# Block transposes and a way over DRAM in place of 32 TensorE transposes, in a hybrid decoder layer

## The chip, the cores and the metric

The kernel runs on one core of one Trainium2 chip. The metric is the device time of one execution in microseconds (us), here the median of three runs. A core has TensorE (PE; its weight loads are listed as PEld), VectorE (DVE), ScalarE (ACT), GpSimd (POOL) and SyncE (SP), and 16 DMA engines that they share. TensorE writes only to PSUM, which has eight banks here, two for each of the tags acc, s, pt and o.

## The reference

One decoder layer over 1040 tokens (16 learned meta tokens ahead of 1024 tokens) of width 1024:

```python
h = concat([meta, x])                               # (1040, 1024)
u = rmsnorm(h, g_pre_mix)
q, k, v, xr, yr = split(u @ w_in)                   # widths 512, 128, 128, 512, 512
attn = sliding_window_attention_with_sinks(q, k, v) # window 128, 8 heads, 2 kv heads
hr = rg_lru(causal_depthwise_conv(xr))              # gated linear recurrence over time
rec = gelu(yr) * hr
h = h + rmsnorm(concat([attn, rec]) @ w_out, g_post_mix)
f = square(relu(rmsnorm(h, g_pre_ffn) @ w_ff1)) @ w_ff2
out = (h + rmsnorm(f, g_post_ffn))[16:]
```

All inputs and outputs are float32.

## The kernel before

Every float32 operand of a matrix product is split into a high part (rounded to float32r, ScalarE) and a low part (the remainder, VectorE). A product is three matmuls, high by high, high by low and low by high (`mm3`, lines 125, 130 and 131), added up in one PSUM bank.

The change lies in the first stage, the input projection. Its right-hand operand is `u`, kept transposed: eight pairs of tiles (one for each 128 columns of the width, index `kc`), 1040 tokens wide. It is made in four pieces of tokens, `ALL = [(0, 272), (272, 256), (528, 256), (784, 256)]`. Piece 0 holds the meta tokens and x tiles 0 and 1 (128 tokens each); piece `b` holds x tiles `2b` and `2b + 1`. The x tiles are loaded early by SyncE into eight buffers of tag c (`load_x`, line 147), which later hold other things.

To make a piece, `norm_rows` (line 254 the square with its sum on ScalarE, lines 170 and 176 the power on POOL, line 260 the scaling on VectorE) writes a normalised tile into one of four buffers of tag d. `transposed` (line 357) then has TensorE transpose each 128x128 block of it against an identity matrix into a PSUM bank, the tags pt, o and s in turn, and `split_scaled` (lines 117 and 118) evicts the bank with the gain `g_pre_mix` as the scale: ScalarE writes the high part of `u`, VectorE the low part.

The loop over `b` at line 498 then runs four projections on each piece: k, v, the first pair of q heads and the first quarter of x_rec, each 24 matmuls of 256 columns into an acc bank (`project`, `part`), with an eviction (`sink_k` line 433 and 437, `sink_v` 464, `sink_q` 476 and 479, `sink_x` 490). `done[b]` keeps the transposes of piece `b` behind the projections of piece `b - 2`, in order alone.

The order of instructions on each engine is not written by hand. A planner simulates the program and picks, for each engine, the ready instruction with the highest priority (program order, with a few exceptions); it also adds every semaphore. Buffers of one tag are handed out as they come free. On the chip each engine then runs its list in order, and SyncE's DMAs are issued in the order of its list. After the first stage SyncE loads the weights of later projections (line 208) and the gate weights (line 794).

Of the kernel before, what the change touches and what calls it, by code (L numbers as in the profile page):

```python
# [9 lines left out]
F32 = mybir.dt.float32  # L10
F32R = mybir.dt.float32r
AF = mybir.ActivationFunctionType
ALU = mybir.AluOpType
# [3 lines left out]
P = 128  # L17
D = 1024
KC = D // P
# [18 lines left out]
def hybrid_layer(  # L38
# [6 lines left out]
    nc = tc.nc  # L45
# [4 lines left out]
    small = ctx.enter_context(tc.tile_pool(name="small", bufs=4))  # L50
    slab = ctx.enter_context(tc.tile_pool(name="slab", bufs=1))
    ps = ctx.enter_context(tc.tile_pool(name="ps", bufs=2, space=PSUM))
    dpool = ctx.enter_context(tc.tile_pool(name="dpool", bufs=1, space=DRAM))
# [4 lines left out]
    def slot(tag, shape, dt=F32):  # L58
        uid[0] += 1
        return slab.tile(shape, dt, tag=tag, name=f"{tag}{uid[0]}", bufs=bufs[tag])  # L60

    def pair(tag, shape):
        return slot(tag, shape, F32R), slot(tag, shape, F32R)

    def bank(tag, shape=(P, 512)):
        uid[0] += 1
        return ps.tile(list(shape), F32, tag=tag, name=f"ps_{tag}{uid[0]}")

    def f32(ap):
        return ap.bitcast(F32)  # L70
# [35 lines left out]
    def behind(name, *inss):  # L106
        for ins in inss:
            tc.add_manual_dep(
                ins, name,
                mybir.DependencyInfo(  # L110
                    mybir.DependencyClass.NoSync, mybir.DependencyReason.DATA
                ),
                reason="order",
            )

    def split_scaled(hi, lo, src, scale):
        high = nc.scalar.activation(hi, src, AF.Copy, scale=scale).ins
        low = nc.vector.scalar_tensor_tensor(
            lo, src, scale, f32(hi), op0=ALU.mult, op1=ALU.subtract
        ).ins  # L120
        return high, low
# [21 lines left out]
    xt = []  # L143
# [18 lines left out]
    g_mix_col, g_ffn_col = gcol[:, 0:8], gcol[:, 8:16]  # L162
# [4 lines left out]
    def rstd_of(ssq_parts, n=P):  # L167
        ms = small.tile([P, 1], F32, name="ms", tag="ms")
        if len(ssq_parts) == 1:
            nc.gpsimd.tensor_scalar(ms[:n], ssq_parts[0], EPS, None, op0=ALU.add)  # L170
        else:
            nc.vector.scalar_tensor_tensor(
                ms[:n], ssq_parts[0], EPS, ssq_parts[1], op0=ALU.add, op1=ALU.add
            )
        rs = small.tile([P, 1], F32, name="rs", tag="rs")
        last_pow[0] = nc.gpsimd.tensor_tensor(
            rs[:n], ms[:n], half_pow[:n], op=ALU.pow
        ).ins.name
        return rs[:n]
# [49 lines left out]
    u = [pair("a", [P, TT]) for _ in range(KC)]  # L229
    RMS_SC = 1.0 / math.sqrt(D)  # L230

    def norm_first(src, halves):

        xn = slot("d", [P, D])
        ss = [small.tile([P, 1], F32, name=f"hq{i}", tag=f"hq{i}") for i in range(2)]
        c = slice(0, 512 if halves else D)
        nc.scalar.activation(
            xn[:, c], src[:, c], AF.Square, scale=RMS_SC, accum_out=ss[0]
        )
        if halves:  # L240
            c = slice(512, D)
            nc.vector.tensor_tensor_reduce(
                out=xn[:, c], in0=src[:, c], in1=src[:, c], scale=RMS_SC * RMS_SC,
                scalar=EPS, op0=ALU.mult, op1=ALU.add, accum_out=ss[1],
            )
        rs = root_rstd(ss[0], ss[1] if halves else eps_col)
        for c in (slice(0, 512), slice(512, D)):
            nc.vector.tensor_scalar(xn[:, c], src[:, c], rs, None, op0=ALU.mult)
        return xn

    def norm_rows(src, n, link=False):
        xn = slot("d", [P, D])
        ssq = small.tile([P, 1], F32, name="ssq", tag="ssq")
        ins = nc.scalar.activation(
            xn[:n], src, AF.Square, scale=RMS_SC, accum_out=ssq[:n]
        ).ins
        if link:
            chained(0, ins)
        rs = rstd_of([ssq[:n]], n)
        ins = nc.vector.tensor_scalar(xn[:n], src, rs, None, op0=ALU.mult).ins  # L260
        if link:
            chained(1, ins)
        return xn
# [24 lines left out]
    ALL = [(0, 272), (272, 256), (528, 256), (784, 256)]  # L288
# [17 lines left out]
    def load(n, cols, after=None):  # L306
        for _ in range(n):
            ins = nc.tensor.matmul(
                idle[:, :cols], zeros[:, :P], zeros[:, :cols], start=True, stop=True,
                skip_group_check=True,  # L310
            ).ins
            if after:
                behind(after, ins)
        return ins.name
# [4 lines left out]
    def normed(b):  # L319
        if b == 0:  # L320
            return [
                (norm_rows(meta_t[:NMETA], NMETA), NMETA),
                (norm_first(xt[0], True), P), (norm_first(xt[1], False), P),
            ]
        rows = [(xt[2 * b], P), (xt[2 * b + 1], P)]
        return [(norm_rows(s[:m], m), m) for s, m in rows]
# [4 lines left out]
    def chained(e, ins):  # L331
        if last[e] is not None:
            behind(last[e], ins)
        last[e] = ins.name
# [12 lines left out]
    def low_w(w, raw):  # L347
        chained(1, nc.vector.tensor_tensor(w[1], raw, f32(w[0]), op=ALU.subtract).ins)

    def transposed(b, xn, after=None):  # L350
        t0, n = ALL[b]
        for kc in range(KC):
            flip[0] += 1
            pt = bank(("pt", "o", "s")[flip[0] % 3])
            o = 0
            for s, m in xn:
                ins = nc.tensor.transpose(
                    pt[:, o : o + m], s[:m, kc * P : (kc + 1) * P], ident[:m, :m]
                )
                if after:  # L360
                    behind(after, ins.ins)
                o += m
            if b == 0:
                load(1, P, ins.ins.name)
            uh, ul = u[kc]
            if b == 0 and kc in (0, 1):
                key_casts.pop(0)()
            high = split_scaled(
                uh[:, t0 : t0 + n], ul[:, t0 : t0 + n], pt[:, :n],
                g_mix_col[:, kc : kc + 1],  # L370
            )
            if b == 0:
                chained(0, high[0])
                chained(1, high[1])

    def fetch(cols, tag="raw", pieces=1):
        raw = slot(tag, [P, KC, P])
        o = 0
        for lo, n in cols:
            src = w_in[:, lo : lo + n].rearrange("(k p) c -> p k c", p=P)  # L380
            for i in range(pieces):
                ks = slice(KC // pieces * i, KC // pieces * (i + 1))
                nc.sync.dma_start(raw[:, ks, o : o + n], src[:, ks])
            o += n
        return raw
# [6 lines left out]
    xn = normed(0)  # L392
# [70 lines left out]
    def sink_v(acc, t0, n):  # L463
        ins = nc.scalar.copy(vt[:, t0 : t0 + n], acc).ins
        if t0 == 0:
            chained(0, ins)
# [28 lines left out]
    done = [None, None]  # L495
    q0, sink_q0 = new_q()
    xr0, sink_x0 = new_x("c")
    for b in range(4):
        if b:
            transposed(b, xn if b == 1 else normed(b), done[b])  # L500
        piece = ALL[b]
        if b == 0:

            acc = [bank("acc"), bank("acc")]
            for a, w in zip(acc, (wk, wv)):
                part(a, w, piece, 0)
                part(a, w, piece, 1)
            xn = [(norm_rows(xt[2], P, True), P)]
            xn.append((norm_rows(xt[3], P, True), P))
            part(acc[0], wk, piece, 2)  # L510
            sink_k(acc[0][:, : piece[1]], *piece)
            part(acc[1], wv, piece, 2)
            sink_v(acc[1][:, : piece[1]], *piece)
            wx = high_w(rx)
            low_w(wx, rx)
            for w, (t0, n), sink, tag in (
                (wq, (16, 256), sink_q0, "o"), (wx, piece, sink_x0, "acc"),
            ):
                acc = bank(tag)
                for k in range(3):  # L520
                    part(acc, w, (t0, n), k)
                sink(acc[:, :n], t0, n)
            done.append(last_mm[0])
            continue
        project(wk, [piece], sink_k)
        project(wv, [piece], sink_v)
        project(wq, [piece], sink_q0)
        project(wx, [piece], sink_x0)
        done.append(last_mm[0])
    for h in range(2):  # L530
        r, o, m = HALF[h], HALF[1 - h], slice(P - NMETA, 2 * P)
# [62 lines left out]
    for b in range(2):  # L594
        pv = bank("pt", (P, 4, P))
        for i in range(4):
            o = NMETA + (4 * b + i) * P
# [288 lines left out]
    for cs in ((0, 1), (2, 3)):  # L886
# [13 lines left out]
        for c in cs:  # L900
            for half in range(2):
                y = ys[c][:, 512 * half : 512 * half + 512]
# [400 lines left out]
    done = set()  # L1303
# [205 lines left out]
```

## Time and profile before

| what | value |
|---|---|
| device time, median of 3 runs | 956.22 us (954.28 to 958.12) |
| span of the profiled execution | 955.3 us |
| device time of the profiled execution | not given apart from its span |
| bytes from and to HBM | 109.93 MB read, 18.87 MB written |
| DMAs issued by SyncE between 28 and 65 us | none |

The span runs from the first to the last instruction of the profiled execution. Busy time is the time that an engine had an instruction at work; a line number is that of the source line (often of a helper) that issued it. In the timeline each row gives the start, the duration and the operation, and in brackets the idle time ahead of it with what ended it.

### The profile page before, as it was taken

Reading aid. Unit: us, or ns where it says so; the run is one execution under the profiler, and the core shown is the slowest. Engines: PE = TensorE matmul, PEld = TensorE weight load, DVE = VectorE, ACT = ScalarE, POOL = GpSimd, SP = SyncE. Lnnn points to the kernel's source line nnn. Section 1 sums busy time; section 2 is a strip of 40 time slices with the busy share of each in tenths; the row PEclk is TensorE's granted clock in tenths of the full one; section 3 lists DMA queues with packets and bytes.
Section 4 is the critical chain, followed back from the end, with each engine's and each line's share of the span. In section 5 each row is a group of like instructions: output and inputs, shape, how many; then the busy total and the mean of one; then the engine's idle time right before and its main releaser. Section 6 shows DMA issues by size and latency. Waiting matters only on the chain.

```text
span 955.3 us, 12432 instructions
## 1 busy us (share of the span) xinstructions
PE 943.8 (99%) x4728; PEld 789.7 (83%) x4728; DVE 655.7 (69%) x845; ACT 505.9 (53%) x854; POOL 129.1 (14%) x189
## 2 busy tenths in 40 slices
PE   9999999999999999999999999999999999999996
PEld 8999999877888878888888888888887788888885
DVE  6567987788856787665644465476667576779893
ACT  7537766568645554444655575654433343446441
POOL 4102563520021100010000000001121100001201
PEclk9999999999999999999999999999999999999999
DMA  8221010204226368674422364334777765647934
GB/s 271 56 67 23 24 45 24 67 23 131 83 109 185 133 220 264 198 253 144 155 89 88 111 203 127 104 113 114 175 180 186 185 199 177 192 139 196 246 65 89
DMA packets 88199, 130.21 MB, mean 136 GB/s; under 512 B 13702, under 2 KB 52630, under 8 KB 88140
## 3 DMA queue, kind: packets, MB, share of 16 engines
q1 hardware_dynamic: 78972, 104.44, 34.0%
q0 software_dynamic: 8880, 24.19, 12.2%
q8 instruction: 37, 0.61, 0.3%
q10 hardware_dynamic: 288, 0.79, 0.2%
q14 instruction: 22, 0.18, 0.1%
HBM read 109.93 MB, written 18.87 MB: 135 GB/s over the span
## 4 chain that ended last, share of the span: by engine, by line
PE 88%; DVE 5%; ACT 3%; DMA 2%; POOL 1%; issue 1%; SPq 0%; DVEq 0%; ACTq 0%; POOLq 0%
PE ps_acc L130 10%; PE ps_acc L131 10%; PE ps_acc L125 10%; PE ps_s L131 6%; PE ps_s L130 6%; PE ps_s L125 6%; PE ps_pt L130 6%; PE ps_pt L131 6%; PE ps_pt L125 6%; PE ps_o L130 5%; PE ps_o L131 5%; PE ps_o L125 5%; ACT c L82 1%; PE ps_o L691 1%; PE ps_acc L282 1%
## 5 line engine op out<-in xcount | busy, mean ns | idle before, releaser
L99 DVE TENSOR_TENSOR ws<-raw,ws 128x1024 fp32r<-128x1024 f32 (+1 forms) x69 | 82.6, 1197 | 76.1 <-ACT ws L96 24.3
L96 ACT CAST ws<-raw 128x1024 fp32r<-128x1024 f32 (+1 forms) x68 | 69.7, 1026 | 87.9 <-PE ps_o L130 23.9
L96 ACT CAST ws<-e 128x1024 fp32r<-128x1024 f32 x41 | 43.0, 1049 | 82.8 <-PE ps_o L130 35.3
L125 PE MATMUL ps_acc<-a,ws 128*128 128x256 f32 (+2 forms) x256 | 85.8, 335 | 0.0
L130 PE MATMUL ps_acc<-a,ws 128*128 128x256 f32 (+2 forms) x256 | 85.5, 334 | 0.0
L131 PE MATMUL ps_acc<-a,ws 128*128 128x256 f32 (+2 forms) x256 | 85.0, 333 | 0.0
L99 DVE TENSOR_TENSOR b<-b,b 128x1024 fp32r<-128x1024 f32 (+2 forms) x50 | 58.9, 1177 | 24.8 <-PE ps_o L130 19.1
L96 ACT CAST b<-b 128x1024 fp32r<-128x1024 f32 (+2 forms) x49 | 49.9, 1019 | 46.4 <-DVE b L996 41.0
L99 DVE TENSOR_TENSOR ws<-e,ws 128x1024 fp32r<-128x1024 f32 x41 | 50.1, 1223 | 32.4 <-ACT ws L96 18.9
L680 POOL TENSOR_SCALAR_AFFINE_SELECT c<-c 128x512 fp32r<-128x512 f32 x64 | 53.6, 858 | 67.6 <-ACT c L96 59.3
L125 PEld LDWEIGHTS ps_acc<-a,ws 128*128 128x128 f32 x256 | 48.3, 189 | 4.7 <-issue 0.2
L131 PEld LDWEIGHTS ps_acc<-a,ws 128*128 128x128 f32 x256 | 48.3, 189 | 4.5
L130 PEld LDWEIGHTS ps_acc<-a,ws 128*128 128x128 f32 x256 | 48.2, 188 | 4.4 <-issue 0.4
L125 PE MATMUL ps_acc<-ws,b 128*128 128x512 f32 (+1 forms) x120 | 46.3, 387 | 1.1 <-ACT ws L96 1.1
L130 PE MATMUL ps_acc<-ws,b 128*128 128x512 f32 (+1 forms) x120 | 46.3, 386 | 0.5 <-DVE ws L99 0.4
L131 PE MATMUL ps_acc<-ws,b 128*128 128x512 f32 (+1 forms) x120 | 46.1, 385 | 0.0
L125 PE MATMUL ps_pt<-ws,b 128*128 128x512 f32 x112 | 44.4, 396 | 0.0
L130 PE MATMUL ps_pt<-ws,b 128*128 128x512 f32 x112 | 44.1, 394 | 0.0
L131 PE MATMUL ps_pt<-ws,b 128*128 128x512 f32 x112 | 44.0, 393 | 0.0
L125 PE MATMUL ps_s<-ws,b 128*128 128x512 f32 x110 | 43.4, 395 | 0.0
L131 PE MATMUL ps_s<-ws,b 128*128 128x512 f32 x110 | 43.3, 394 | 0.0
L130 PE MATMUL ps_s<-ws,b 128*128 128x512 f32 x110 | 43.3, 393 | 0.0
(416 smaller groups left out, 2662.0 us busy)
## 6 DMA issues: line engine op xcount, KB each, us to landing
raw<-in_w_ff_dram SPq DMA_DIRECT2D x61, 512.0 KB, 4.1
e<-in_w_ff_dram SPq DMA_DIRECT2D x45, 512.0 KB, 4.0
a<-in_w_ff_dram SPq DMA_DIRECT2D x12, 512.0 KB, 6.6
s_dram<-a POOLq DMA_DIRECT2D x12, 512.0 KB, 3.7
c<-in_x_dram SPq DMA_DIRECT2D x8, 512.0 KB, 4.0
raw<-in_w_in_dram SPq DMA_DIRECT2D x8, 512.0 KB, 3.7
d<-in_x_dram SPq DMA_DIRECT2D x8, 512.0 KB, 3.3
out_dram<-raw SPq DMA_DIRECT2D x8, 512.0 KB
```

What stands on the lines that cost most here:

```text
L82: ins = nc.scalar.activation(*args, **kwargs).ins
L96: nc.scalar.copy(hi, src)
L99: low = nc.vector.tensor_tensor(lo, src, f32(hi), op=ALU.subtract).ins
L125: ins = nc.tensor.matmul(dst, lh, rh, start=start, stop=False, skip_group_check=True).ins
L130: nc.tensor.matmul(dst, lh, rl, start=False, stop=False, skip_group_check=True)
L131: last_mm[0] = nc.tensor.matmul(dst, ll, rh, start=False, stop=stop, skip_group_check=True).ins.name
L282: last_mm[0] = nc.tensor.matmul(acc[:, :n], w[k // 2][:, kc, :], u[kc][k % 2][:, t0 : t0 + n], start=k == 0 and kc == 0, stop=k == last an ...
L680: nc.gpsimd.affine_select(out=p_[:, :, s], in_=f32(p_[:, :, 0]), pattern=[[0, 4], [g, P]], compare_op=op, fill=0.0, base=0, channel_multip ...
L691: nc.tensor.matmul(po[:, oc : oc + n], v, p_[:, pc : pc + n], start=first and k == 0, stop=last and k == 1, skip_group_check=True,)
```

## The change

For the tiles of pieces 2 and 3, the transposition is done in two steps without TensorE. VectorE turns each 32x32 block of a normalised tile in place (one instruction over 128x1024), and two sets of DMAs put the blocks where they belong: four writes per tile (runs of 1 KB) into a DRAM scratch, and eight reads per tile (one for each `kc`, 512 runs of 128 bytes each) back into the buffers that the x tiles had. `split_scaled` then reads SBUF instead of PSUM. Both sets are issued by SyncE. The normalisation of piece `b + 1` with its DMAs stands in the program ahead of the projections of piece `b`. Pieces 0 and 1 are as before.

```diff
+    x_dram = dpool.tile([4, 4, P, 2 * P], F32, name="x_dram")
+
+    def blocks(y, src, dram):
+        nc.vector.transpose(
+            y.rearrange("p (b k t) -> p b k t", b=4, k=KC),
+            src.rearrange("p (k b d) -> p b k d", k=KC, b=4),
+        )
+        for a in range(4):
+            nc.sync.dma_start(
+                dram[a].rearrange("(b d) r -> d b r", b=4),
+                y[32 * a : 32 * a + 32].rearrange("p (b r) -> p b r", b=4),
+            )
+
+    def unblock(dst, dram, kc):
+        nc.sync.dma_start(
+            dst.rearrange("p (a t) -> p a t", a=4),
+            dram[:, :, 32 * kc : 32 * kc + 32].rearrange("a p t -> p a t"),
+        )
+
+    def norm_blocks(b):
+        for i in (2 * b, 2 * b + 1):
+            src, y = xt[i], slot("d", [P, D])
+            ssq = small.tile([P, 1], F32, name="ssq", tag="ssq")
+            nc.scalar.activation(y, src, AF.Square, scale=RMS_SC, accum_out=ssq)
+            rs = rstd_of([ssq])
+            nc.vector.tensor_scalar(src, src, rs, None, op0=ALU.mult)
+            blocks(y, src, x_dram[i - 4])
+
+    def read_blocks(b):
+        for i in (2 * b, 2 * b + 1):
+            for kc in range(KC):
+                o = 256 * (kc % 4) + P * (i % 2)
+                unblock(xt[2 * b + kc // 4][:, o : o + P], x_dram[i - 4], kc)
+
+    def split_blocks(b):
+        t0, n = ALL[b]
+        for kc in range(KC):
+            uh, ul = u[kc]
+            o = 256 * (kc % 4)
+            split_scaled(
+                uh[:, t0 : t0 + n], ul[:, t0 : t0 + n],
+                xt[2 * b + kc // 4][:, o : o + n], g_mix_col[:, kc : kc + 1],
+            )
...
     for b in range(4):
-        if b:
-            transposed(b, xn if b == 1 else normed(b), done[b])
+        if b == 1:
+            transposed(b, xn, done[b])
+        elif b:
+            split_blocks(b)
+        if b in (1, 2):
+            norm_blocks(b + 1)
+            read_blocks(b + 1)
         piece = ALL[b]
```

## The prediction

> **What bounds the kernel now.** I read the page first (busy time, then the chain that ended last), then the busy time of each engine in windows of 10 us, then the timeline of TensorE around the place of the change, and last the issue costs of the DMAs.
>
> ```profile
> span 955.3 us, 12432 instructions
> PE 943.8 (99%) x4728; PEld 789.7 (83%) x4728; DVE 655.7 (69%) x845; ACT 505.9 (53%) x854; POOL 129.1 (14%) x189
> PE 88%; DVE 5%; ACT 3%; DMA 2%; POOL 1%; issue 1%; SPq 0%; DVEq 0%; ACTq 0%; POOLq 0%
> ```
>
> TensorE is busy in all but 11.5 us (955.3 - 943.8) and holds 88% of the chain, so matrix work taken out is worth its full time as long as nothing else arrives late. The windows (columns: length, then busy us and instruction count of PE, PEld, DVE, ACT, POOL; granted clock; DMA share; GB/s) show what lies beside the four projection pieces:
>
> ```profile
> 20.00:30.00 10.00, 10.00 (x84) 9.64 (x83) 8.78 (x19) 7.51 (x17) 4.36 (x12) 1.00 0.62 159
> 30.00:40.00 10.00, 10.00 (x88) 10.00 (x88) 5.00 (x12) 4.55 (x13) 0.76 (x2) 1.00 0.01 2
> 40.00:50.00 10.00, 10.00 (x88) 10.00 (x86) 5.01 (x11) 5.21 (x14) 0.78 (x2) 1.00 0.01 2
> 50.00:60.00 10.00, 10.00 (x87) 9.81 (x86) 5.44 (x24) 2.91 (x10) 2.16 (x3) 1.00 0.08 18
> ```
>
> From 30 to 60 us TensorE is full while VectorE and ScalarE are half idle and the DMA engines nearly unused. From 20 to 30 us VectorE is nearly full as well (8.78 of 10). The change loads VectorE in the first of these windows and the DMA queue in the others.
>
> **What goes: 32 TensorE transposes.** Pieces 2 and 3 have two tiles each with eight 128x128 transposes. One run of eight, between two projections:
>
> ```profile
> 33.56 0.36 PE L125 MATMUL ps_acc<-a,ws 128*128 128x256 f32 x1
> ...
> 39.18 0.29 PE L131 MATMUL ps_acc<-a,ws 128*128 128x256 f32 x1
> 39.31 0.38 PE L357 MATMUL ps_s<-ident,d 128*128 128x128 f32 x2
> ...
> 40.07 0.27 PE L357 MATMUL ps_o<-ident,d 128*128 128x128 f32 x1
> 40.10 0.36 PE L125 MATMUL ps_acc<-a,b 128*128 128x256 f32 x1
> ...
> 53.45 0.37 PE L125 MATMUL ps_acc<-a,b 128*128 128x256 f32 x1
> ```
>
> Two projections of 24 matmuls run from 33.56 to 39.18: 47 steps, 0.12 us each; one projection is then 24 x 0.12 = 2.9 us and a piece of four 11.5 us. The eight transposes start at 39.31 and the last at 40.07, 0.76 us for seven steps: 0.11 us each. Thirty-two are 3.5 us. That is the whole gain that the change can have on TensorE itself: 0.37% of the run, under the 0.5% (4.8 us) that a measurement of this kernel can tell from no change. The 16 evictions by `split_scaled` stay in number and size and read SBUF instead of PSUM; I cost that at nothing, since VectorE and ScalarE are half idle there; without that cover it would be tenths of a microsecond.
>
> **What comes: a chain that must keep up.** In place of a transpose right behind the normalised tile stands: square on ScalarE, power on POOL, scaling on VectorE, a block transpose on VectorE (1), four DMA writes, their landing, eight DMA reads per tile, their landing, then the two splits. The last tile of piece 2 is tile 5; its scratch slot (tag d) comes free only when piece 1's transposes have read theirs, as before:
>
> ```profile
> 27.20 1.06 ACT L254 ACTIVATE d<-c 128x1024 f32<-128x1024 f32 x1
> 29.36 0.76 DVE L260 TENSOR_SCALAR d<-c,rs 128x1024 f32<-128x1024 f32 x1
> 39.77 0.48 ACT L117 ACTIVATE a<-ps_s,gcol 128x256 fp32r<-128x256 f32 x1
> 40.29 0.48 DVE L118 SCALAR_TENSOR_TENSOR a<-ps_s,gcol,a 128x256 fp32r<-128x256 f32 x1 [1.96 <-ACT a L117]
> L99 DVE TENSOR_TENSOR ws<-raw,ws 128x1024 fp32r<-128x1024 f32 (+1 forms) x69 | 82.6, 1197 | 76.1 <-ACT ws L96 24.3
> ```
>
> So tile 5 is scaled at 29.36 + 0.76 = 30.1. No block transpose is in this trace. The nearest rows over 128x1024 f32 are the scaling (0.76 us) and the two-input subtraction (1.20 us); I take 1.2, since its strided source speaks for the slower row, and 2.4 as an upper bound. Tile 5 is turned at 31.3. The two splits at the far end take 0.48 + 0.48 = 0.96 us.
>
> The DMAs are all issued by SyncE, in order, 12 per tile and 24 per piece. SP is empty from 27.9 to 65.3 before, so nothing else of the kernel queues behind them:
>
> ```profile
> L383 SPq DMA_DIRECT2D raw<-in_w_in_dram x3: 405/503/507, 2.9 to 3.9; - x3
> L794 SPq DMA_DIRECT2D e<-in_w_a_dram x2: 627/760/892, 25.0 to 25.9; - x2
> L794 SPq DMA_DIRECT2D e<-in_w_x_dram x2: 607/610/614, 26.6 to 27.3; - x2
> 26.63 1.26 SPq L794 DMA_DIRECT2D e<-in_w_x_dram  x2
> 65.28 3.24 SPq L208 DMA_DIRECT2D raw<-in_w_in_dram  x3
> raw<-in_w_in_dram SPq DMA_DIRECT2D x2, 256.0 KB, 3.0
> ws<-ws POOLq DMA_DIRECT2D x2, 36.0 KB, 2.0
> DMA packets 3591, 1.16 MB, mean 232 GB/s; under 512 B 2566, under 2 KB 3590, under 8 KB 3590
> q1 hardware_dynamic: 3590, 1.15, 92.0%
> ```
>
> (Columns of the first three: ns to issue one, min/median/max. The seventh and the eighth row end in KB and us from issue to landing. The last two are the DMA engines from 25 to 30 us.) A read of the change has four runs per partition, as L383's has on as many partitions (0.41 to 0.51 us) and L794's on half as many with runs nearer in size (0.61 to 0.89). I take p = 0.55 us an issue, between 0.50 and 0.61, and keep 0.41 and 0.89 as the ends. For landing I take 2.2 us from issue for 64 and 128 KB, between 2.0 at 36 KB and 3.0 at 256 KB.
>
> Piece 2: from 31.3 the queue passes four writes of tile 5, the four reads of tile 4 that go into tile 5's buffer (they must wait for its block transpose), and eight reads of tile 5: 16 x 0.55 = 8.8, so the last read is issued at 39.55, lands at 41.75, is split at 42.7, and its last matmul (0.28) ends at 43.0. Before, that projection ended at 40.10 + 2.9 = 43.0. TensorE would be ready for it at 39.3 - 12 x 0.11 = 38.0: the transposes taken out turn into a wait of about the same size.
>
> Piece 3: the same queue then passes eight writes and sixteen reads, 40 issues after 31.3 in all. The last read is issued at 31.3 + 39p, lands 2.2 later, is split 0.96 later, and its last matmul takes 0.28: 34.74 + 39p. Before, that projection ended at 53.45 + 2.9 = 56.3. The difference is 39p - 21.6, which is -0.1 us at p = 0.55. It cannot fall under -3.5 (the transposes), reached at p = 0.46. Each 0.05 us of issue cost is worth 2 us.
>
> **VectorE ahead of piece 1.** Tile 4's block transpose comes right behind its scaling:
>
> ```profile
> 21.31 0.75 DVE L260 TENSOR_SCALAR d<-c,rs 128x1024 f32<-128x1024 f32 x1 [0.76 <-DMA d<-in_b_a_dram]
> 21.98 0.85 DVE L437 TENSOR_TENSOR b<-ps_acc,b 64x256 fp32r<-64x256 f32 x2
> ...
> 25.73 0.48 DVE L118 SCALAR_TENSOR_TENSOR a<-ps_pt,gcol,a 128x256 fp32r<-128x256 f32 x1
> 26.47 0.36 PE L130 MATMUL ps_acc<-a,b 128*128 128x256 f32 x1
> ```
>
> From 21.98 to 25.73 VectorE has no gap, and piece 1's second matmul (26.47) stands right behind its first low part (25.73 + 0.48 = 26.21). A block transpose put in at 22.0 is queued ahead of all of it and moves TensorE by up to 1.2 us; put in after the splits it costs nothing. I take half, 0.6, bounds 0 and 1.2 (2.4 if one takes twice as long). The other three fall where VectorE is half idle.
>
> Sum: -3.5 (transposes) + 3.4 (new waits before pieces 2 and 3) + 0.6 (VectorE) = +0.5 us on a span of 955.3. The page gives no device time of the profiled execution apart from that span; the median is 956.2, 0.9 over it, and the three runs go from 954.3 to 958.1. Added to the median: 956.7.
>
> **Rivals.** *Hidden* (the chain keeps up): p at 0.46 or less, as the cheapest L383 row (0.41) allows, and the block transpose in a gap. Then all 3.5 us are gained: 952.7. For it: SP and DMA engines are empty there. Against it: only one of L383's three rows is that cheap, and all four of L794's are over 0.6.
>
> *The SP queue is the bound* (slower). Place: 24 issues per piece against 11.5 us of matmuls per piece, so the queue is the longer one from p = 0.48 on, and only the head start hides it. With p = 0.75, inside L794's span of 0.61 to 0.89, 39p - 21.6 = 7.7, with VectorE's 0.6 8.3: 964.5. It passes 0.5% from p = 0.66 on ((4.8 - 0.6 + 21.6) / 39). For it: the runs of 128 bytes are smaller than any of L794's, and four issues of the nearest size all cost over 0.6. Against it: issues with 128 partitions cost less in L383's rows. The Trainium skill (TensorE: Matmul & The Clock Gate, Part 1) says that TensorE's clock falls to half when it idles through a window of about 3.4 us; the waits of this case would be that long, and its first matmuls, 0.24 in place of 0.12 us each, would add an estimated 1.7 us. The windows above grant 1.00 throughout, so no row here bears it out or contradicts it.
>
> *The packets are the bound* (slower). From 25 to 30 us 3590 packets took 92% of 16 engines: 0.92 x 16 x 5 / 3590 = 20.5 ns each at 0.32 KB. A read is 512 packets, 32 an engine, 0.66 us at that price: about the issue cost, so it hardly matters. At twice that, 1.31 us, the 28 reads after 31.3 take 36.7, with twelve writes at 0.55 6.6, so with 2.9 us for the end the last matmul is done at 77.5, 21 us late: 978. The Trainium skill (DMA: Bandwidth & Descriptors, Specifications) names 512 B as the least transfer for line rate, with a read-modify-write below. Against it: two thirds of the packets in that window (2566 of 3591) are under 512 B and show no such price.
>
> *The plan behind it moves.* Instructions are ordered by a planner's simulated times, and fewer PSUM tiles in the rotation of three shift the later ones. Only 11.5 us of idle TensorE are there to win; I give a gain of about 6 us in all (950) a small chance.
>
> **How the numbers follow.** Forecast 0.45 (own range 953.5 to 960, p from 0.47 to 0.63 with VectorE at 0.6), hidden 0.17, SP queue 0.28, packets 0.05, plan 0.05. Faster by over 0.5% is the last alone: 0.05. Within 0.5% are forecast and hidden: 0.62. Slower are SP queue and packets: 0.33. The range of 952.4 to 966 leaves out the plan (0.05), the packets (0.05) and the SP queue above p = 0.79 (0.06).
>
> **What the profile of the changed kernel would show.** Right: 40 instead of 72 transposes at TensorE; four block transposes near 1.2 us; 48 more DMAs on SP between 22 and 54 us, 0.5 to 0.6 us apart; gaps of TensorE of some 2 us ahead of the first matmuls of pieces 2 and 3, ended by VectorE or ScalarE that waited for a DMA. No such gaps would mean hidden; gaps that grow from piece 2 to piece 3, with SP issuing without pause, the SP queue; SP pausing while the DMA share is full, the packets. I am wrong if p lies outside of 0.47 to 0.63, if landing takes 3 us or more, or if the order of the queue differs (tile 6 ahead of tile 5).

## The result, and the profile after

The changed kernel takes 961.88 us (median of 4 runs, 959.98 to 963.71) against 955.94 us for the kernel before beside it (954.28 to 958.12): a ratio of 1.0063, 95% interval 1.0043 to 1.0084. A second comparison of the same two kernels gave 961.13 against 955.77 us, ratio 1.0048 (1.0029 to 1.0067). It is slower by some 0.55%. The forecast of 956.7 was 5.2 us too low, and the time lies above the forecast's own range (953.5 to 960). Its likeliest outcome, within 0.5% of before, was missed in the first comparison (0.63%) and just met in the second (0.48%). The wide range of 952.4 to 966 held the time, but only because it made room for the SP queue rival, which is not what happened.

The page of the profiled execution (963.71 us of device time, so 2.0 over its span): span, busy times, and the chain that ended last.

```profile
span 961.7 us, 12461 instructions
PE 945.9 (98%) x4696; PEld 789.3 (82%) x4696; DVE 660.6 (69%) x849; ACT 507.3 (53%) x854; POOL 129.5 (13%) x189
PE 88%; DVE 3%; DMA 2%; ACT 2%; SPq 2%; issue 1%; POOL 1%; DVEq 0%; ACTq 0%; POOLq 0%
```

TensorE has 32 instructions fewer (4696 for 4728), and it now stands idle for 15.8 us (961.7 - 945.9) where it was 11.5. The four windows of the first stage (columns as in the prediction):

```profile
20.00:30.00 10.00, 8.95 (x73) 8.50 (x73) 8.89 (x19) 6.76 (x17) 3.75 (x11) 1.00 0.68 193
30.00:40.00 10.00, 10.00 (x86) 9.67 (x85) 8.67 (x16) 4.61 (x12) 3.56 (x6) 1.00 0.62 121
40.00:50.00 10.00, 8.73 (x66) 7.91 (x65) 7.81 (x34) 5.22 (x13) 0.00 (x0) 1.00 0.80 174
50.00:60.00 10.00, 9.86 (x82) 9.51 (x81) 4.40 (x10) 4.79 (x11) 0.00 (x0) 1.00 0.62 106
```

Three of them have lost TensorE time that was full before. The first loss is at 25 us. The timeline of VectorE and TensorE there:

```profile
23.61 1.25 DVE L379 STREAM_TRANSPOSE d<-c 128x1024 f32<-128x1024 f32 x1
24.78 1.18 DVE L348 TENSOR_TENSOR ws<-e,ws 128x1024 fp32r<-128x1024 f32 x1
...
26.02 1.26 PE L282 MATMUL ps_acc<-a,ws 128*128 128x272 f32 x8 [1.05 <-DVE ws L348]
```

Tile 4's block transpose stands ahead of the low part of wx (L348), and TensorE waits for that low part: 1.33 us from the last start to the next where a step is 0.12, so 1.2 us lost. Then SP's queue:

```profile
23.20 2.07 SPq L208 DMA_DIRECT2D raw<-in_w_in_dram  x3
25.38 2.32 SPq L384 DMA_DIRECT2D x_dram<-d  x4
30.64 2.28 SPq L390 DMA_DIRECT2D c<-x_dram  x4
33.02 2.54 SPq L384 DMA_DIRECT2D x_dram<-d  x4
35.60 6.52 SPq L390 DMA_DIRECT2D c<-x_dram  x12
42.23 3.87 SPq L384 DMA_DIRECT2D x_dram<-d  x8
46.26 9.40 SPq L390 DMA_DIRECT2D c<-x_dram  x16
```

From 33.02 to 55.66 it issues 40 DMAs with hardly a pause: 0.566 us each. What waits for them, and a wait of another kind between (ScalarE's and TensorE's rows; the bracket is the idle time and its cause):

```profile
40.45 1.54 ACT L117 ACTIVATE a<-c,gcol 128x256 fp32r<-128x256 f32 x3 [1.32 <-DMA c<-x_dram]
41.01 0.19 PEld L125 LDWEIGHTS ps_acc<-a,b 128*128 128x128 f32 x1 [0.35 <-ACT a L117]
...
47.54 0.75 ACT L477 CAST b<-ps_acc 64x256 fp32r<-64x256 f32 x2 [2.90 <-PE ps_acc L131]
48.30 0.37 ACT L508 COPY c<-ps_acc 128x256 f32<-128x256 f32 x1
48.73 0.39 PE L125 MATMUL ps_acc<-a,ws 128*128 128x256 f32 x1 [0.99 <-ACT c L508]
...
61.87 0.39 PE L125 MATMUL ps_acc<-a,ws 128*128 128x256 f32 x1 [0.66 <-ACT c L508]
```

Ahead of piece 2 TensorE waits for splits that waited for reads (about 1.2 us over some matmuls). The planner has woven the k and the v projection of the piece together, so that TensorE finds work in the waits (probably because the data comes a column at a time). But then both end at nearly the same time and hold both acc banks, and the q projection waits for the evictions of k (L477) and v (L508): 1.27 us from start to start at 47.45, again 0.94 at 60.93. From the first matmul of wx to the same matmul behind the first stage (22.51 to 66.62 us before, 22.59 to 68.56 after) the steps of TensorE over 0.17 us hold 6.3 us of lost time, each counted over 0.12, against 1.4 in the kernel before: 5.0 more. The rest of that stretch is 3.1 us shorter by the transposes taken out, and 5.0 less 3.1 is the 1.9 us by which TensorE is late.

To see where the rest went I matched the instructions of VectorE, ScalarE and GpSimd of each profile with those of the kernel before and took the median lag in stretches of 20 us. One execution each; the last column is the median of the runs less that of the kernel before timed beside it. All kernels of the experiments below are in it (in us, minus is earlier):

| kernel | lag near 70 us | near 700 | near 780 | median of the runs |
|---|---|---|---|---|
| before, once more | 0.1 | 0.9 | -0.4 | |
| changed | 1.9 | 2.4 | 6.3 | +5.9 |
| changed, once more | 4.0 | 4.5 | 7.6 | +5.4 |
| dve_late | 5.6 | 6.3 | 5.5 | +7.4 |
| no_trip | 1.8 | 2.3 | 0.7 | +2.3 |
| no_trip_ordered | -1.7 | -1.0 | -0.8 | -1.4 |
| idle_trip | 6.9 | 6.9 | 4.7 | +5.9 |
| q_bank | 2.5 | 3.0 | 2.8 | +4.3 |
| few_reads | 2.8 | 3.3 | 2.5 | +3.3 |
| weights_late | 3.9 | 4.6 | 3.4 | +4.1 |
| weights_late_q_bank | 0.9 | 2.0 | 3.8 | +3.1 |
| piece3_only | -0.8 | -0.2 | 0.5 | +1.3 |
| piece3_ahead | -1.6 | -1.0 | 1.2 | +0.3 |

What is lost or won before 70 us stays to 700 us within about 1 us. Between 700 and 780 us the profiles gain or lose up to 4 us in one place, the kernel before too. There TensorE waits for a weight that ScalarE splits late because its load came late. The same row of the waits from 735 to 775 us, first of the kernel before:

```profile
PEld ps_acc L125 <- ACT ws L96: 1.5, 1, 1.5
```

and of the changed kernel:

```profile
PEld ps_acc L125 <- ACT ws L96: 3.6, 1, 3.6
```

This late step makes the first profile look 4 us worse than its first stage was. The same row in the second profile of the changed kernel and in that of the kernel before:

```profile
PEld ps_acc L125 <- ACT ws L96: 3.1, 1, 3.1
PEld ps_acc L125 <- ACT ws L96: 0.7, 1, 0.7
```

Behind the two long waits TensorE's granted clock is 0.50, for 6.83 us from 761.32 in the first profile and for 3.41 us from 765.53 in the second; behind the short ones it stays at 1.00. So the late wait was long in both profiles of the changed kernel and short in both of the kernel before. That the change brings it is not shown: among the kernels below that also make all 48 DMAs it goes from none (`idle_trip`) to 2.9 us (`weights_late_q_bank`), and the times of the kernel before alone range over 5 us. Where the medians stand 5.9 and 5.4 us over the kernel before's, the first stage explains 1.9 and 4.0 of the two profiles; the cause of the rest, 1.4 to 4.0 us, is open.

### The profile page after: what moved, and what is told of

It reads as the page before. It is cut to its first block, busy times and chain, and to the rows that moved or that the text cites. A ratio compares the mean times of both kernels' runs of the same rounds, so it can differ in the third digit from the quotient of the medians.

```text
span 961.7 us, 12461 instructions
## 1 busy us (share of the span) xinstructions
PE 945.9 (98%) x4696; PEld 789.3 (82%) x4696; DVE 660.6 (69%) x849; ACT 507.3 (53%) x854; POOL 129.5 (13%) x189
## 4 chain that ended last, share of the span: by engine, by line
PE 88%; DVE 3%; DMA 2%; ACT 2%; SPq 2%; issue 1%; POOL 1%; DVEq 0%; ACTq 0%; POOLq 0%
PE ps_acc L130 10%; PE ps_acc L125 10%; PE ps_acc L131 10%; PE ps_s L131 6%; PE ps_s L125 6%; PE ps_s L130 6%; PE ps_pt L130 6%; PE ps_pt L131 6%; PE ps_pt L125 6%; PE ps_o L125 5%; PE ps_o L131 5%; PE ps_o L130 5%; PE ps_o L740 1%; SPq L390 1%; POOL c L729 1%
```

## The experiments

Each kernel is the changed one with the edit shown, timed beside the kernel before.

**The changed kernel and the kernel before again** (`again`, `before_again`).

> The changed kernel once more, for a second profile and more times. In its first profile it loses 1.9 us against the kernel before by 65 us of the span and nothing more up to 740 us; between 740 and 765 us it loses another 4.1, where weight loads of the last product land late. Theory A (the late loss belongs to the change, by a shift of what the DMA engines meet): ratio to before 1.005 to 1.008 again, and a TensorE wait of 2 us or more near 757 us in the profile. Theory B (the late loss is a matter of luck of single executions): in some profile of this kernel or of the kernel before it goes the other way, and the times scatter by 4 us.

> The kernel before once more, for a second profile. Theory A: the wait of TensorE near 755 us is about 1.1 us again, as in the first profile. Theory B: it can be 3 us or more.

961.13 us; the kernel before 956.52 in its one profiled run. The two theories are not decided. A's wait came (3.01 us from start to start at 761 us), its ratio just not (1.0048); the kernel before waited 0.3 us, neither A's 1.1 nor B's 3; and the times of the changed kernel spread over 5 us, as B says. The second profile of the changed kernel differs from the first ahead of piece 2: tile 4's reads begin at 31.73 us in place of 30.64, and TensorE's wait there is 2.00 us from start to start. The lag near 70 us is 4.0 in place of 1.9: the waits for the data of pieces 2 and 3 lost 4.2 us in place of 1.8, so they alone differ by over 2 us between executions.

**No way over DRAM** (`no_trip`).

```diff
-            blocks(y, src, x_dram[i - 4])
...
-            read_blocks(b + 1)
```

> Leaves out the block transposes and the way over DRAM: the splits of pieces 2 and 3 read the scaled tiles as they lie, so u holds other data there. What is left is the removal of 32 TensorE transposes alone. If the chain over VectorE, SP and DRAM is what cost the first 1.9 us, this gains about 3.5 us by 65 us of the span against the kernel before (lag -3.3 to -3.7). The late stage: theory A in the form that the 48 added DMAs or the scratch tensor do it: no late loss, 0.9965 of before; theory A in the form that the fewer instructions of TensorE (or the different PSUM rotation) do it: late loss there too, 1.000 of before.

958.02 us, ratio 1.0013 (1.0001 to 1.0026): slower than the kernel before with 32 transposes fewer and no wait for data. The planner used the freedom: it pulled the splits of pieces 2 and 3, ready at 22 us, in among those of piece 1. Two of TensorE's waits in its timeline:

```profile
26.47 0.38 PE L125 MATMUL ps_acc<-a,b 128*128 128x256 f32 x1 [0.55 <-ACT a L117]
...
38.65 0.38 PE L125 MATMUL ps_acc<-a,ws 128*128 128x256 f32 x1 [0.89 <-ACT c L506]
```

The waits cost the clock as well. Two windows (columns as in the prediction; the granted clock is the third number from the end):

```profile
25.35:28.76 3.41, 1.36 (x8) 0.74 (x6) 3.32 (x8) 3.37 (x10) 1.81 (x6) 1.00 1.09 282
28.76:32.17 3.41, 3.11 (x15) 3.12 (x16) 3.41 (x10) 3.41 (x9) 1.12 (x2) 0.50 0.09 17
```

So it did not measure the removal alone. It showed that the order of VectorE and ScalarE from 22 to 31 us, with the clock that it cost, is worth as much as the transposes, and that the wait for the evictions comes without any DMA.

**No way over DRAM, order kept** (`no_trip_ordered`).

```diff
             high, low = split_scaled(...)
+            behind(v_out[b - 1], high)      # v eviction of the piece before
```

> The changed kernel without the block transposes and without the way over DRAM (pieces 2 and 3 split the scaled tiles as they lie, so u holds other data there), and with the splits of each of these pieces held behind the eviction of the v projection of the piece before it, so that the planner can't pull them in among piece 1's splits. What is left of the change is that 32 TensorE transposes are gone. Theory 'saving and waits apart': the whole 32 x 0.11 = 3.5 us show, the instructions at 65 us stand 3.0 to 3.7 us earlier than in the kernel before, 952 to 953.5 us at the end (the late part scatters by some us on single runs). Rival 'the transposes lay beside other waits': they are gone and next to nothing is gained, a lag between -1 and 0 at 65 us and 955 to 956 us.

954.22 us, ratio 0.9984 (0.9973 to 0.9995), the instructions 1.7 us earlier near 70 us: faster, but half of what was expected. VectorE's timeline shows most of the other half: two scalings of 0.75 us, no longer tied to a buffer of tag d, stand ahead of piece 1's low parts.

```profile
24.37 0.75 DVE L400 TENSOR_SCALAR c<-c,rs 128x1024 f32<-128x1024 f32 x1
25.15 0.86 DVE L525 SCALAR_TENSOR_TENSOR b<-ps_o,b 64x256 fp32r<-64x256 f32 x2
26.04 0.75 DVE L400 TENSOR_SCALAR c<-c,rs 128x1024 f32<-128x1024 f32 x1
...
27.36 0.44 PE L357 MATMUL ps_pt<-ident,d 128*128 128x128 f32 x2 [0.80 <-DVE a L118]
```

The largest steps of TensorE here are 0.48 and 1.07 us at 25.68 and 26.29, and one of 0.56 us at 34.61. Counted as for the changed kernel, its steps lose 2.74 us against 1.38 in the kernel before. These 1.36 us and the 1.70 that TensorE is early at the end make 3.1: the saving is real, and a little smaller than the 3.5 of the forecast.

**Tile 4's block transpose behind piece 1's low parts** (`dve_late`).

```diff
         ins = nc.vector.transpose(...).ins
+        if low_1:                       # last low part of piece 1
+            behind(low_1.pop(), ins)
```

> The changed kernel with the block transpose of tile 4 held behind the low parts of piece 1 on VectorE. If it is that transpose that makes TensorE wait 1.2 us near 25 us (24.69 to 26.02), that wait goes, and the lag at 65 us falls from 1.9 to about 0.7. If piece 2's data are then later by as much (tile 4's four writes and first reads start some 6 us later), the waits at 41 and 48 us take it back, and the lag stays at 1.9.

963.17 us, ratio 1.0059 (1.0038 to 1.0079), and a lag of 5.6 us near 70, worse than either expectation. The wait at 25 us is gone, and a longer one has come ahead of piece 2, because the writes of tile 4 are now issued at 30.11 and all 16 reads follow tile 5's writes (timeline of SP's queue, L390 the writes and L396 the reads, and of TensorE):

```profile
30.11 1.80 SPq L390 DMA_DIRECT2D x_dram<-d  x4
...
33.66 1.98 SPq L390 DMA_DIRECT2D x_dram<-d  x4
35.76 8.69 SPq L396 DMA_DIRECT2D c<-x_dram  x16
...
43.20 0.72 PE L125 MATMUL ps_acc<-a,b 128*128 128x256 f32 x2 [3.95 <-ACT a L117]
```

Behind that wait the granted clock is 0.50 from 43.31 to 46.72 us. In this order VectorE's 1.25 us came back only at the price of later data.

**The trip made, nobody waiting for it** (`idle_trip`): pieces 2 and 3 by TensorE, all DMAs still issued.

```diff
-            split_blocks(b)
+            transposed(b, [(xt[2 * b], P), (xt[2 * b + 1], P)], done[b])
...
-                unblock(xt[2 * b + kc // 4][:, o : o + P], x_dram[i - 4], kc)
+                unblock(spare[i - 4][:, P * kc : P * kc + P], x_dram[i - 4], kc)
```

> The changed kernel with pieces 2 and 3 turned by TensorE as before, and the whole trip (four block transposes, 16 writes, 32 reads) still made beside it; the reads land in the tile that the block transpose wrote, and nobody uses them. Theory 'saving and waits apart': of the trip's cost only VectorE's 1.25 us ahead of the low part of wx at 25 us is left, because nobody waits for the data: the instructions at 65 us stand 0.8 to 1.8 us later than in the kernel before, 956.6 to 957.6 us. Rival 'the 48 transfers cost by themselves' (the queue's later loads of weights come late, or the transfers slow others): 3 us and more at 65 us, 959 us or more.

961.59 us, lag 6.9 us: a miss by its end, and the experiment's own doing. Up to 35 us the lag was 1.0, VectorE's term alone, as expected. Then the square of tile 7 on ScalarE, which had no part in TensorE's path, waited for a buffer of tag d that the idle trip's DMAs still held (the row names a write out of one), and with it everything behind it in ScalarE's order:

```profile
41.68 1.06 ACT L401 ACTIVATE d<-c 128x1024 f32<-128x1024 f32 x1 [5.08 <-DMA x_dram<-d]
...
44.52 0.55 PE L125 MATMUL ps_acc<-a,b 128*128 128x256 f32 x1 [3.19 <-DVE b L525]
```

The granted clock then fell to 0.50 for 6.83 us from 43.29, a second part of the lag. So it doesn't settle the price of the transfers by themselves; ahead of 41 us TensorE has no wait due to them.

**The q projection in a third bank** (`q_bank`).

```diff
-        project(wq, [piece], sink_q0)
+        project(wq, [piece], sink_q0, "acc" if b == 1 else "o")
```

> The changed kernel with the q projection of pieces 2 and 3 summed in the o bank (free there, as no transposes use it) in place of the two acc banks. Theory 'the eviction wait is a part of its own': the gaps of 1.27 and 0.94 us at 47.5 and 61 us, where the next projection waited for the evictions of k and v that end together, go or fall below 0.4 us each; at 65 us the instructions stand 1.5 to 2.2 us earlier than in the changed kernel (there 1.9 and 4.0 us behind the kernel before in its two profiles), 959 to 960 us at the end. Rival 'the data sets the end of each piece': the same time is spent in waits for the reads instead, no change, 961 to 962 us.

959.93 us, ratio 1.0037 (1.0025 to 1.0049). Both waits for the evictions are gone: no step over 0.25 us is left between 43.2 and 65 us. The wait for piece 2's data is as long as in the second profile of the changed kernel (2.19 us at 40.39 us, there 2.00), and against that profile the lag is 1.5 us less, although the clock fell behind this wait; against the first profile it is 0.6 us more. A wait of 0.80 us is new at 33.73. The eviction wait is a part of its own: it goes without the data wait going. The median stands 4.3 us over the kernel before's, where the changed kernel's two stand 5.9 and 5.4 over theirs.

**One read for both tiles** (`few_reads`).

```diff
-            dst.rearrange("p (a t) -> p a t", a=4),
+            dst.rearrange("p (a t) -> p a t", a=8),   # blocks of tiles i and i + 1
...
```

> The changed kernel with each read from DRAM fetching a column of blocks of both tiles of the piece (128x256 in place of 128x128): 16 reads in place of 32, of the same bytes in the same packets of 128 B. Theory 'SP's issues pace the data': a read still costs the queue 0.55 to 0.65 us, the 16 issues of piece 3 (9.4 us) become 8 in 4.5 to 5 us, piece 2's data is complete 3 us earlier, and at 65 us the instructions stand 1.5 to 3 us earlier than in the changed kernel: 958 to 960 us. Rival 'the packets pace the data' (a read kept the DMA engines busy for 0.505 us of its 0.566): a read now takes 1.0 us or more, the 8 of piece 3 take 8 us or more, piece 2's reads all start behind tile 5's writes and end no earlier, and it is 961 to 963 us.

959.44 us, ratio 1.0035 (1.0023 to 1.0047). Its queue's timeline, the reads of pieces 2 and 3:

```profile
37.26 5.62 SPq L391 DMA_DIRECT2D c<-x_dram  x8
...
48.76 6.43 SPq L391 DMA_DIRECT2D c<-x_dram  x8
```

Twice the bytes cost 0.70 and 0.80 us a read on average, where the 40 DMAs of the changed kernel had taken 0.566 each: between the two expectations. (The 0.505 us that the expectation gives to the DMA engines is a read's time on SP's queue; of the engines a read took 0.41 us, worked out below, so twice the bytes are 0.83, about what a merged read cost.) The share of the DMA engines (the sum of their packets' times over 16 engines, so it can pass 1) went to 1.17 from 40 to 45 us, where it had been 0.81. The median stands 3.3 us over the kernel before's, 2.0 to 2.6 less than the changed kernel's, but the profile does not show the issue theory's way there. All reads of piece 2 stand behind tile 5's writes and are issued by 42.88 us (42.12 and 43.40 in the changed kernel's two profiles), as the rival said; they land 3.0 to 3.7 us after issue; a wait of 1.17 us came ahead of piece 3; and the lag of 2.8 near 70 us lies between the changed kernel's 1.9 and 4.0. The issues got cheaper and the data came no earlier, so what they are worth in time is not shown.

**The later weights behind the reads of piece 2** (`weights_late`).

```diff
             ins = nc.sync.dma_start(raw[:, :, o : o + n], ...).ins
+            behind(read[2], ins)
```

> The changed kernel with the loads of the later projections' weights (three of them issued at 23 us, first read at 63 to 65 us) held on SP's queue behind the reads of piece 2; nothing else. Theory 'the writes of tile 4 land late because their packets stand behind these loads': the writes of tile 4 land within 2.5 us of their issue and its reads start at 28 to 29 us and not at 30.6 to 32.5; they no longer stand beside tile 5's writes, the wait ahead of piece 2 (1.1 to 4.2 us with its lower clock) falls below 0.5 us; at 65 us the instructions stand 1 to 3 us earlier than in the changed kernel, 958 to 960.5 us. Rival 'tile 5's chain or the issues set it': the first reads start earlier, but piece 2's last data comes when it did, 961 to 962 us.

960.22 us, ratio 1.0042 (1.0029 to 1.0055). Its queue's timeline (L387 the writes, L393 the reads):

```profile
24.80 1.81 SPq L387 DMA_DIRECT2D x_dram<-d  x4
28.53 2.04 SPq L393 DMA_DIRECT2D c<-x_dram  x4
33.09 1.78 SPq L387 DMA_DIRECT2D x_dram<-d  x4
34.92 7.59 SPq L393 DMA_DIRECT2D c<-x_dram  x12
```

The writes of tile 4 now land 1.9 us after the last was issued (26.61 to 28.53), where it was 2.9 (27.70 to 30.64): the weights had stood ahead of them, with the DMA engines' share at 1.07 from 25 to 30 us. (These three loads are issued at 23 us, inside the first stage, in the kernel before too.) In the second profile of the changed kernel it was 4.3 us (27.47 to 31.73). But the plan lets only four reads of tile 4 go ahead of tile 5's writes, and SP stands from 30.6 to 33.1 for tile 5's block transpose. Piece 2's data came no earlier, and TensorE's wait ahead of it was 1.49 us where less than 0.5 was expected: the rival was right on that. The planner also put norms ahead of piece 1's last splits, and a wait of 1.15 us for evictions opened at 34.4.

**Both** (`weights_late_q_bank`).

> Both: the loads of the later weights held behind the reads of piece 2, and the q projection of pieces 2 and 3 in the o bank. Theory 'data waits and eviction waits add up': both of them are gone or small, what is left is -3.5 us for the transposes and +1.25 us for VectorE ahead of the low part of wx: at 65 us the instructions stand 1 to 2.3 us earlier than in the kernel before, 953.5 to 956 us. Rival 'the projections wait for the data whichever bank they use': a wait of 2 us or more stays ahead of piece 2 or 3, and it is 958 us or more.

959.26 us, ratio 1.0035 (1.0022 to 1.0047). The lag near 70 us is 0.9, the least of the kernels with both pieces by blocks, but not the gain expected: of the steps over 0.3 us three are left, 1.32 at 24.67 (VectorE), 1.27 at 34.02 (those evictions) and 1.42 at 53.12 (piece 3's data). The late wait was long in this profile (2.87 us, the clock at 0.50 behind it) and took its lag to 3.8.

**Piece 3 alone by blocks** (`piece3_only`).

```diff
-        if b == 1:
-            transposed(b, xn, done[b])
+        if b in (1, 2):
+            transposed(b, xn if b == 1 else normed(b), done[b])
```

> Piece 2 turned by TensorE as before, piece 3 alone by block transposes and DRAM, with some 15 us more between its tiles and its first projection than piece 2 had. Theory 'saving and waits apart': 16 transposes x 0.11 = 1.75 us are saved, the block transposes don't stand ahead of piece 1's low parts, and the data is there in time: 1.2 to 2.0 us earlier than the kernel before at 65 us, 953.8 to 955 us. Rival 'the trip brings its wait wherever it is': TensorE waits for reads or VectorE ahead of piece 3 for 2 us or more, 956.5 to 959 us.

956.92 us, ratio 1.0014 (1.0002 to 1.0025): still a little slower than the kernel before. No wait at 25 us; the lag is -0.5 us at 30 and -0.8 at 70, where -1.2 to -2.0 was expected. One wait of 1.36 us is left at 52.14, for the data: tile 7's square waited for a d buffer, so its writes began only at 41.31.

**The same, arranged** (`piece3_ahead`): merged reads; piece 2's tiles scaled in place; the order of piece 3's steps fixed. Of the edit, the lines that set the order:

```diff
+        behind(v_out[1] if i == 7 else gate[2], sq)      # squares
+        behind(gate[0], ...)                             # scalings: last low part of piece 1
+        behind(gate[i % 2], ins)                         # block transposes
```

> Piece 2 by TensorE as before, piece 3 alone by blocks, arranged by what the runs so far showed: one read a column of blocks for both tiles (8 reads in place of 16), the norms, the block transposes and the splits of piece 3 held behind piece 1's splits (tile 7's norm behind piece 1's v eviction, piece 3's splits behind piece 2's v eviction), and piece 2's tiles scaled in place, so that no d buffer is waited for. Theory 'saving and waits apart': no wait at 25 us, piece 3's data complete by 47 to 49 us where TensorE wants it at 51, so that the gap of 1.36 us of piece3_only goes: the instructions at 65 us stand 1.4 to 2.0 us earlier than in the kernel before, 953.5 to 954.6 us, 0.1 to 0.2% faster. Rival 'any insertion into the plan brings a wait of its own' (an eviction or a norm that stands in another place on ScalarE or VectorE): 0.5 us or more of new gaps, between -1 and +1 us at 65 us, 955 to 957 us.

956.03 us, ratio 0.9999 (0.9986 to 1.0012): no difference. Up to 280 us the instructions stand 1.5 to 1.6 us earlier, as expected. The gap ahead of piece 3 did not go, though: a step of 0.79 us is left at 51.94, now ended by the eviction of x_rec, which is the rival's sign. Between 720 and 780 us the profiled execution lost all of it and more in the wait for a late weight, 3.16 us where the kernel before has 1.48. The waits from 735 to 775 us and the windows around it:

```profile
PEld ps_acc L125 <- ACT ws L96: 3.2, 1, 3.2
```

```profile
755.00:760.00 5.00, 2.24 (x8) 1.22 (x7) 1.92 (x2) 3.00 (x4) 0.00 (x0) 0.88 0.60 159
760.00:765.00 5.00, 5.00 (x19) 4.00 (x18) 3.89 (x4) 0.89 (x1) 0.00 (x0) 0.77 0.67 212
```

That wait ends at 758.10 us, in the kernel before at 758.17. Whether the weight stream always takes an early gain back there or whether this execution had a late load is open: `no_trip_ordered`, just as early, kept 0.8 us behind it and a faster median. Of all versions only `no_trip_ordered` is measurably faster than the kernel before, and it leaves out part of the work.

## Why the prediction was right or wrong

The range held the time, and not by the forecast's account: the sum of +0.5 us came out at +1.9 and +4.0 in the first stage, and as much as 4 us arose behind it, for which the sum has no term.

**Transposes, -3.5: right in kind, 3.1 in size.** 40 are left at TensorE. The run of eight that the prediction shows goes from 39.31 to the next matmul at 40.10, 0.79 us or 0.10 each, since the last step is short; the difference of the traces is 3.1, and `no_trip_ordered` shows the same. Nor is 0.5% the least that can be told from no change: that kernel's 0.16% is clear of it.

**VectorE, 0.6: too low by half.** I had taken the middle of 0 to 1.2. The transpose was put in ahead, and the whole of it came through. Its price was right: 1.24 to 1.25 us for all four where 1.2 was taken.

```profile
L379 DVE STREAM_TRANSPOSE d<-c x4: 1236/1245/1245, 23.6 to 36.2; 128x1024 f32<-128x1024 f32 x4
```

There was no reason for the middle: no gap stood between 21.98 and 25.73, and `dve_late` shows that the other end is no better.

**The queue, p = 0.55: right; its start: 1.7 us too early.** The 40 issues took 0.566 each, and the formula 39p - 21.6 gives 0.5 us for that. (One of the three L383 loads that it was taken from has eight runs per partition, not four.) But tile 5's writes began at 33.02, not at 31.3, since its scaling stood at 30.60 (before 29.36), late like all that followed the wait at 25 us; it was turned at 31.39 to 32.64. Landing of a read, 2.2 taken, was 2.5 to 2.6 in the first profile and 2.3 to 4.1 in the second, where landings are on record:

```profile
L390 SPq DMA_DIRECT2D c<-x_dram x32: 367/506/927, 30.6 to 55.2; - x32
DMA to landing us min/median/max: 2.5/2.6/2.6
```

The last read of piece 3 started at 55.2 where 31.3 + 39p had said 52.8.

**New waits, 3.4: near in the first profile, wrong in kind.** In the first profile the waits of pieces 2 and 3 lost 3.8 us: 1.8 for the data and 2.0 for evictions of k and v; in the second 6.2: 4.2 and 2.0. The eviction part was not in the prediction, so that 3.4 is near 3.8 is luck. I had k end at 43.0 in the kernel before and v follow. Its evictions of k and v in piece 2 show that the two were partly woven there already:

```profile
44.99 0.74 ACT L433 CAST b<-ps_acc 64x256 fp32r<-64x256 f32 x2 [3.34 <-PE ps_acc L131]
46.06 0.37 ACT L464 COPY c<-ps_acc 128x256 f32<-128x256 f32 x1 [0.32 <-PE ps_acc L131]
```

In the changed kernel they end together, which hid part of the data wait and made a new one out of the two acc banks. `q_bank` shows it.

**The sum, +0.5:** with the measured terms it is -3.1 + 3.8 + 1.2 = +1.9 in the first profile and -3.1 + 6.2 + 1.2 = +4.3 in the second, where the lag is 4.0. The term that I left out of the sum is the spread of the data waits. In the second profile tile 4's writes landed later behind the weights, its first reads ended at 34.81, and tile 5's writes began only at 34.91, 1.9 us after the first profile's. The loss behind 70 us is a second term that is not in it, and its cause is open.

**Of the rivals,** the SP queue as the bound did not come as told: p stayed under 0.66, and the gaps did not grow from piece 2 to piece 3. Packets did not come either. The DMA engines from 50 to 55 us, where SP issues reads alone:

```profile
q1 hardware_dynamic: 4347, 0.54, 70.0%
```

That is 0.70 x 16 x 5 / 4347 = 12.9 ns a packet where the prediction had 20.5, and 512 packets over 16 engines are 0.41 us a read, less than its 0.5 us on the queue; 1.31 was never near. A test that changes the size of the packets alone was not run. Hidden is what `piece3_only` and `piece3_ahead` come near to in the first stage, with half of the transposes.

The clock sentence did not come true in the first stage of the changed kernel, whose clock is 1.00 there in both profiles; it did in `q_bank`, `dve_late`, `idle_trip` and `no_trip`, and behind the long late waits. Windows of `q_bank` (wait of 2.19 us at 40.39), then of the changed kernel's second profile (2.00 us at 40.32):

```profile
40.24:43.65 3.41, 1.48 (x10) 1.07 (x9) 1.09 (x3) 1.63 (x5) 0.00 (x0) 1.00 0.76 118
43.65:47.06 3.41, 3.41 (x18) 3.41 (x17) 2.77 (x7) 2.42 (x6) 0.00 (x0) 0.50 0.85 197
```

```profile
38.49:41.90 3.41, 2.11 (x18) 1.90 (x17) 1.37 (x5) 0.52 (x3) 0.82 (x1) 1.00 0.75 117
41.90:45.31 3.41, 2.85 (x19) 2.53 (x20) 2.97 (x10) 3.41 (x9) 0.00 (x0) 1.00 0.77 144
```

In `q_bank` sixteen matmuls stand 0.213 us apart from 43.69 to 47.1 in place of 0.118: 1.5 us on top of the wait, where the estimate in the prediction was 1.7. The Trainium skill (TensorE: Matmul & The Clock Gate, Part 1) ties the drop to an idle window of about 3.4 us; the length agrees (3.41 us at 0.50), but the window need not be idle: TensorE was busy for 1.48 us of it in `q_bank`. The 2.00 us of the second profile fell on two such windows, with 2.11 and 2.85 us busy, and the clock stayed.

**What the profile would show:** 40 transposes, four block transposes near 1.2 us and 48 DMAs on SP, the 40 of the long row 0.57 us apart, were all there. The gaps ahead of pieces 2 and 3 were there, but not of 2 us each: 1.2 and 0.6 us were lost in the first profile, 2.6 and 1.6 in the second. The sign I had named as fatal, landing of 3 us or more, was there too: tile 4's writes landed 2.9 and 4.3 us after the last was issued in full, and reads of the second profile up to 4.1 us after issue. I had priced it nowhere.

## What to carry to other kernels

A transposition taken off a full engine is worth its own time only if each step put in its place lands on an engine that is free at that moment: count what stands right behind it in that engine's order, not the engine's share over the stage. A data path of many small DMAs on one queue waits for all that the queue issues before its last one, and its first landing for what was queued ahead, so give it a head start longer than both (piece 3 alone had one, or nearly; pieces 2 and 3 together had not). Where an order is planned by a program, expect each inserted or removed step to move others, and hold these in place before reading what the step itself is worth.

## What the runs showed of the hardware that I had not expected

It was not the length of a wait that decided about TensorE's granted clock, but how much of a fixed stretch of 3.41 us was left busy. Ahead of the run's last 20 us, every fall to 0.50 lasts 3.41 us or twice that. Each of the 14 profiles can be divided into stretches of 3.41 us in step with its falls. At full clock, a fall followed every stretch in which TensorE was busy for 0.44 of it or less (0.03 to 0.44 in the eight ahead of the last 20 us), and none in which it was busy for 0.48 or more. So a wait of 2.19 us inside one stretch cost the clock, and one of 2.00 us over two stretches did not; in `no_trip` several waits of at most 1.38 us from start to start were enough. One stretch at 0.50 then cost 1.5 us of matmuls in `q_bank`.

Four writes of 128 KB, issued behind 2 us of weight loads, landed 2.9 and 4.3 us after the last of them in two profiles, and 1.9 us with these loads held back. Reads of 64 KB in runs of 128 bytes took the queue 0.54 to 0.59 us each, merged ones of 128 KB in the same runs 0.70 to 0.80 us.
